# State space stage of a two-layer trunk: the response matrices' loads move from GpSimd's queue into SyncE's, between weights and output matrices

## The chip, the core and the metric

The kernel runs on one core of a Trainium2 chip. Its engines are TensorE (PE; its weight loads are PEld), VectorE (DVE), ScalarE (ACT), GpSimd (POOL) and SyncE (SP), which here only issues transfers. Transfers run on 16 DMA engines. SP issues into a hardware queue (q1 in the profile), POOL into a software queue (q0). The metric is the device time of one execution in microseconds (us), the median over several; less is better.

## The reference

Two layers over 256 positions of width 2048, each of them `x += mixer(norm(x))`, `x += attention_to_memory(norm(x))`, `x += mlp(norm(x))`, and a last norm. The mixer of layer 0 is a gated MLP, that of layer 1 the state space layer that the change is in:

```
u = (h @ w_in).reshape(bsz, seq, 128, 16)        # 128 groups of 16 channels
bu = einsum('gpc,bsgc->sbgp', b_bar, u)          # 64 complex states a group
states[s] = lam_bar * states[s - 1] + bu[s]      # associative scan over the positions
y = einsum('gcp,sbgp->bsgc', cmat, states).real + d_skip * u
y = gelu(y.reshape(bsz, seq, 2048))
val, gate = split(y @ w_out + b_out, 2)
x = x + val * sigmoid(gate)
```

Everything is float32, `w_in` is 2048 x 2048, `w_out` 2048 x 4096.

## The kernel before, in words

**Weights.** Every large matmul streams its weights in chunks of 512 KB (`wload`, line 127, issued by SP into `wraw`, four buffers). ScalarE casts a chunk to `whi` (line 103), VectorE subtracts to get the remainder `wlo` (line 104), and PE multiplies both (`gemm_tok`, line 159). A load waits until VectorE has split the chunk four back, so SP spends most of its time waiting for buffers. Eight chunks make one piece of 512 columns. The state space stage has 32 chunks of `b_w_in` (numbers 0 to 31, four pieces n = 0 to 3) and 64 of `b_w_out` (32 to 95).

**The scan in matrices.** The positions are cut into blocks of 8 (`T`). Inside a block the output is a product with a response matrix (names `Kd` in HBM, `dq` on chip); what crosses a block goes through states: `pq` (from `Pd`) makes a block's contribution to the state, `carry` runs the recurrence over the blocks, and `qq` (output matrices, from `Qd`) makes outputs from states. All three sorts are worked out by VectorE and PE beside layer 0's MLP and stored in HBM. For each column piece n there are four tiles of each: `pq` and `qq` 512 KB, one transfer each; `dq` 320 KB in four transfers of 32, 64, 96 and 128 KB, as the matrix is zero in steps and its zeros are set once (line 1279). The four dq tiles (`resp`) have one buffer each, so dq of piece n waits until PE has read dq of piece n - 1.

**Order.** `self.at(k, f)` has f issued k chunks after the place where it stands; `self.tick` runs after each chunk. `follow(n)` plans for piece n, whose chunks are just through: `inputs` (transposes, copies to `us`, line 1324), `own` (matmuls with pq, line 1337), `states`, `carry`, `outputs(n, 0)` after 14 chunks and `outputs(n, 1)` after 16, each of them 16 blocks' matmuls with dq (line 1384, 32 matmuls) and then with qq (line 1392, 64 matmuls); for pieces 2 and 3 a chunk or so earlier or later. PE takes this work between the chunks of later pieces.

**Queues.** `load` in `s5` issues on POOL, or with `stream` on SP, behind the last weight load that was issued so far (`issue_after(self.fed)`, line 1272). Before, pq and dq go on POOL (line 1274) and qq on SP; dq of piece 0 is asked for at the start of the stage, while layer 0's MLP still runs, that of later pieces 7 or 8 and 9 or 10 chunks behind their piece.

Of the kernel before, what the change touches and what calls it, by code (L numbers as in the profile page):

```python
# [16 lines left out]
P = 128  # L17
# [21 lines left out]
class Trunk:  # L39
# [1219 lines left out]
    def s5(self, x, cur, nxt):  # L1259
# [3 lines left out]
        with tc.tile_pool(name="s5", bufs=2, reuse_waits="tile") as sp:  # L1263
# [5 lines left out]
            def load(src, out, stream=False):  # L1269
                if stream:  # L1270
                    with tc.issue_after(self.fed):
                        nc.sync.dma_start(out=out, in_=src)
                else:
                    nc.gpsimd.dma_start(out=out, in_=src)
# [6 lines left out]
            def fetch(nm, n, i, stream=False):  # L1281


                if nm == "pq":
                    t = sp.tile([P, 2, 4, P], F32, name=nm, bufs=4)
                    load(self.Pd[4 * n + i], t, stream)
                elif nm == "qq":
                    t = sp.tile([P, 2, 4 * P], F32, name=nm, bufs=4)
                    load(self.Qd[4 * n + i].rearrange("l p r n -> (l p) r n"), t, stream)
                else:  # L1290
                    t, kd = resp[i], self.Kd[4 * n + i]
                    for h in range(4):
                        load(bass.AP(tensor=kd.tensor, offset=kd.offset + 6 * P,
                                     ap=[[P, 2], [(2 * T - 1) * P, 16], [1, 2 * (h + 1) * P]]),
                             t[32 * h:32 * h + 32, 2 * (3 - h) * P:])
                ahead[nm, n, i] = t

            def chunks(n, acc):
# [17 lines left out]
            def inputs(n):  # L1316
                u = st[n].pop()
                us = sp.tile([P, 8, 4, NC], F32, name="us")
                st[n] += [us]
                for h in range(2):  # L1320
                    pt = self.ps([P, 4, P])
                    for l in range(4):
                        nc.tensor.transpose(pt[:, l, :], u[:, 4 * h + l].rearrange("p j c -> p (j c)"), self.ident)
                    nc.scalar.copy(out=us[:, 4 * h:4 * h + 4].rearrange("p l t c -> p l (t c)"), in_=pt)

            def own(n):

                us, = st[n]
                z = sp.tile([P, 4, 2, 2, 64], F32, name="z", bufs=1)
                st[n] += [z]  # L1330
                for h in range(2):
                    pz = self.ps([P, 2, 2, 2, 64])
                    for i in range(2):
                        pq = ahead.pop(("pq", n, 2 * h + i))
                        for l in range(2):
                            for t in range(4):
                                nc.tensor.matmul(pz[32 * t:32 * t + 32, i, l].rearrange("p r s -> p (r s)"),
                                                 us[:, 4 * h + 2 * i + l, t, :], pq[:, l, t, :],
                                                 start=(i + l == 0), stop=True, skip_group_check=True)
                    for i in range(2):  # L1340
                        nc.scalar.copy(out=z[:, 2 * h + i], in_=pz[:, i].rearrange("p l r s -> p r l s"))

            def states(n):

                z = st[n].pop()
                vv = sp.tile([P, 2, NC, NQ // 2], F32, name="vv")
                st[n] += [vv]
                nc.vector.memset(vv[:, :, 0, :], 0.0)
                for h in range(2):
                    pt = self.ps([P, 2, 2, 4, NC])  # L1350
                    for i in range(2):
                        for r in range(2):
                            nc.tensor.transpose(pt[:, i, r].rearrange("p t c -> p (t c)"),
                                                z[:, 2 * h + i, r].rearrange("p l s -> p (l s)"), self.ident)
                    for i in range(2):
                        vo = vv[:, :, 1:, :].rearrange("p r c (t l) -> p l r t c", t=4)[:, 2 * h + i]
                        nc.scalar.copy(out=vo, in_=pt[:, i, :, :, 0:NC - 1])

            def carry(n, c, k, by=1):

                vv = st[n][1]
                cs = slice(16 * n, 16 * n + 16)
                p = by // 2
                m1, m2 = (sp.tile([P, 2, 15, 16], F32, name=f"m{i}", bufs=1)[:, :, :k, :] for i in (1, 2))
                at = lambda c, r: vv[:, r, c:c + 2 * by * (k - 1) + 1:2 * by, :]
                t1 = self.TC1[:, p, cs].unsqueeze(1).unsqueeze(1).broadcast_to([P, 2, k, 16])
                t2 = self.TC2[:, p, :, cs].unsqueeze(2).broadcast_to([P, 2, k, 16])
                new = at(c, slice(None))
                nc.vector.tensor_tensor(out=m1, in0=t1, in1=at(c - by, slice(None)), op=ALU.mult)
                nc.vector.tensor_tensor(out=m2, in0=t2, in1=at(c - by, slice(None, None, -1)), op=ALU.mult)  # L1370
                nc.vector.tensor_tensor(out=new, in0=new, in1=m1, op=ALU.add)
                nc.vector.tensor_tensor(out=new, in0=new, in1=m2, op=ALU.add)

            def outputs(n, half):
                us, vv = st[n][:2]
                if half == 0:
                    st[n] += [[self.ps([P, 4, P]) for _ in range(2)]]
                py = st[n][2]
                pair = (2 * half, 2 * half + 1)
                for i in pair:  # L1380
                    dq = ahead.pop(("dq", n, i)).rearrange("p (j t l c) -> p l t j c", j=T, l=2, t=4)
                    for l in range(2):
                        for t in range(4):
                            nc.tensor.matmul(py[l][32 * t:32 * t + 32, i, :], us[:, 2 * i + l, t, :], dq[:, l, t],
                                             start=(i == 0), stop=False, skip_group_check=True)
                for i in pair:
                    qv = ahead.pop(("qq", n, i)).rearrange("p r (j t c) -> p r t j c", t=4, c=16)
                    for r in range(2):
                        for l in range(2):
                            s = slice(64 * l, 64 * l + 64)  # L1390
                            for t in range(4):
                                nc.tensor.matmul(py[l][32 * t:32 * t + 32, i, :], vv[s, r, :, 4 * t + i],
                                                 qv[s, r, t], start=False, stop=(r == 1), skip_group_check=True)
# [18 lines left out]
            def follow(n):  # L1412

                late = n == NCH - 1
                self.at(5 + late, lambda: own(n))
                for i in range(4):
                    if n + 1 < NCH:
                        self.at(5, lambda i=i: fetch("pq", n + 1, i))
                    if n:
                        self.at(7 + late + i // 2 * 2, lambda i=i: fetch("dq", n, i))  # L1420
                        self.at(10 + late + i // 2 * 2, lambda i=i: fetch("qq", n, i, True))
                self.at(4 + late, lambda: inputs(n))
                self.at(6 + late, lambda: states(n))
                self.at(7 + late, lambda: [carry(n, 2, 15), carry(n, 4, 7, 2)])
                self.at(8 + late, lambda: [carry(n, c, 1, 4) for c in (8, 12, 16)])
                self.at(9 + late, lambda: [carry(n, c, 1, 4) for c in (20, 24, 28)])
                self.at(10 + late, lambda: [carry(n, 6, 7, 2), carry(n, 3, 15)])
                gap = n == NCH - 2
                self.at(14 + 1.5 * gap, lambda: outputs(n, 0))
                self.at(16 + gap, lambda: outputs(n, 1))  # L1430
                self.at(16 + gap, lambda: activated(n))
                self.at(17 + gap if n >= NCH - 2 else 19, lambda: features(n))

            for i in range(4):
                fetch("pq", 0, i)
            for i in range(4):
                fetch("dq", 0, i)
                self.at(2 * i + 2, lambda i=i: fetch("qq", 0, i, True))
            for n in range(NCH):
                acc = self.gemm_tok(hT, a["b_w_in"], n)  # L1440
                if n == 0:
                    st["rstd"] = cur.rstd()
                chunks(n, acc)
                follow(n)
# [224 lines left out]
```

## Time and profile before

| what | value |
|---|---|
| median of 3 runs | 2770.2 us (2769.85 to 2771.99) |
| profiled execution | 2772.35 us |
| its span | 2770.2 us |
| granted TensorE clock | 0.999 |
| TensorE busy | 2748.3 us, 99% |
| VectorE, ScalarE, GpSimd busy | 2066.9, 1426.7, 184.9 us |
| DMA | 593.75 MB, mean 214 GB/s |
| state space stage: chunk 0 to 46 | about 1385 to 1548 us |

The span is the time from the first to the last instruction of the profiled execution; times in the rows are from its start. "PE ps L1384 <- DMA dq<-Kd" reads: PE, in the instruction of line 1384 that writes `ps`, waited for the transfer of `Kd` to `dq`. In a row of the timeline stand start, length, engine, line, operation, output and inputs, shapes, how many, and in brackets the idle time before it with what ended it. In a row of the transfers stand their number, the size of one and the median time from issue to landing; "SPq" and "POOLq" say on which queue.

### The profile page before, as it was taken

The page shows a single profiled execution, that of the slowest core. Times are in us where ns is not written, and L with a number is a line of the kernel's source. Part 1 is how long each engine was busy: PE and PEld are TensorE (multiplying, and loading weights), DVE is VectorE, ACT ScalarE, POOL GpSimd, SP SyncE. Part 2 cuts the span into 40 slices and gives each one's busy share as a digit, 9 for nine tenths or more (in the row PEclk, how much of TensorE's full clock was granted, in tenths as well). Part 3 has the DMA queues.
Part 4 walks back from the last instruction along what each step waited for, and adds up shares of the span by engine and source line. Part 5 has one row for each costly group of instructions (what it writes and reads, how often), then busy time and mean ns, then how long its engine had stood idle before and what let it go on. Part 6 is the DMA issues. An engine that isn't in the chain of part 4 may idle for free. (4 is left out here: it accounts for less than half of the span.)

```text
span 2770.2 us, 39500 instructions
## 1 busy us (share of the span) xinstructions
PE 2748.3 (99%) x14966; PEld 2325.4 (84%) x14966; DVE 2066.9 (75%) x2835; ACT 1426.7 (51%) x1822; POOL 184.9 (7%) x331
## 2 busy tenths in 40 slices
PE   9999999999999999999999999999999999999998
PEld 7888888888888888888888788888888888888887
DVE  6865757878888878787577657568767978879685
ACT  5545545655544434444566445446555655546454
POOL 0100000001011111111203100000000000000000
PEclk9999999999999999999999999999999999999999
DMA  8766566457688887886879766564556557575565
GB/s 293 231 199 214 189 193 217 152 160 238 211 281 259 262 258 257 265 259 219 235 239 284 207 203 206 188 213 156 181 165 231 180 171 241 158 246 166 176 212 160
DMA packets 194175, 593.75 MB, mean 214 GB/s; under 512 B 44096, under 2 KB 45168, under 8 KB 193472
## 3 DMA queue, kind: packets, MB, share of 16 engines
q1 hardware_dynamic: 153456, 537.46, 61.1%
q0 software_dynamic: 40000, 52.71, 6.6%
q8 instruction: 117, 1.92, 0.3%
q10 hardware_dynamic: 528, 1.06, 0.1%
q14 instruction: 74, 0.61, 0.1%
HBM read 567.51 MB, written 23.46 MB: 213 GB/s over the span
## 5 line engine op out<-in xcount | busy, mean ns | idle before, releaser
L104 DVE TENSOR_TENSOR wlo<-wraw,whi 128x1024 fp32r<-128x1024 f32 (+1 forms) x857 | 1041.0, 1220 | 434.8 <-ACT whi L103 429.0
L103 ACT CAST whi<-wraw 128x1024 fp32r<-128x1024 f32 (+1 forms) x857 | 899.4, 1051 | 800.2 <-PE acc L910 172.1
L174 PE MATMUL acc<-act,whi 128*128 128x512 f32 x3072 | 740.9, 391 | 0.6 <-DVE act L246 0.6
L174 PEld LDWEIGHTS acc<-act,whi 128*128 128x128 f32 x3072 | 563.1, 188 | 110.6 <-issue 1.4
L179 PEld LDWEIGHTS acc<-act,wlo 128*128 128x128 f32 x3072 | 395.0, 191 | 17.4 <-DVE wlo L104 1.8
L179 PE MATMUL acc<-act,wlo 128*128 128x256 f32 x3072 | 403.3, 283 | 1.3 <-DVE wlo L104 1.0
L159 PE MATMUL acc<-whi,act 128*128 128x512 f32 x1472 | 370.4, 393 | 5.6 <-ACT whi L103 5.5
L159 PEld LDWEIGHTS acc<-whi,act 128*128 128x128 f32 x1472 | 275.2, 189 | 63.6 <-ACT whi L103 6.3
L810 PE MATMUL acc<-whi,act 128*128 128x512 f32 x824 | 222.7, 392 | 0.0
L910 PE MATMUL acc<-whi,hl 128*128 128x512 f32 x544 | 212.7, 391 | 0.0
L909 PE MATMUL acc<-whi,hh 128*128 128x512 f32 x544 | 212.6, 391 | 0.0
L159 PE MATMUL acc<-wlo,act 128*128 128x512 f32 x736 | 197.9, 391 | 0.0
L810 PEld LDWEIGHTS acc<-whi,act 128*128 128x128 f32 x824 | 152.9, 188 | 35.9 <-ACT ends L846 2.2
L159 PEld LDWEIGHTS acc<-wlo,act 128*128 128x128 f32 x736 | 138.6, 188 | 28.9
L912 PE MATMUL acc<-wlo,hh 128*128 128x512 f32 x544 | 145.8, 389 | 0.0
L810 PE MATMUL acc<-wlo,act 128*128 128x512 f32 x412 | 127.2, 391 | 0.2
L190 ACT COPY r<-acc 128x512 f32<-128x512 f32 x64 | 37.6, 587 | 161.9 <-PE acc L174 161.9
L910 PEld LDWEIGHTS acc<-whi,hl 128*128 128x128 f32 x544 | 102.1, 188 | 22.2 <-issue 1.0
L810 PE MATMUL acc<-whi,hh 128*128 128x512 f32 x308 | 120.5, 391 | 0.0
L909 PEld LDWEIGHTS acc<-whi,hh 128*128 128x128 f32 x544 | 102.1, 188 | 21.4 <-issue 0.2
L912 PEld LDWEIGHTS acc<-wlo,hh 128*128 128x128 f32 x544 | 102.0, 188 | 21.4 <-issue 0.2
L810 PE MATMUL acc<-whi,hl 128*128 128x512 f32 x308 | 119.9, 389 | 0.0
(387 smaller groups left out, 2951.3 us busy)
## 6 DMA issues: line engine op xcount, KB each, us to landing
wraw<-in_f_w_up SPq DMA_DIRECT2D x256, 512.0 KB, 4.5
wraw<-in_f_w_down SPq DMA_DIRECT2D x200, 512.0 KB, 5.6
wraw<-in_x_w_q SPq DMA_DIRECT2D x64, 512.0 KB, 3.7
wraw<-in_x_w_k SPq DMA_DIRECT2D x64, 512.0 KB, 4.5
wraw<-in_b_w_out SPq DMA_DIRECT2D x64, 512.0 KB, 4.5
wraw<-in_a_w_in SPq DMA_DIRECT2D x63, 512.0 KB, 4.7
wraw<-in_x_w_o SPq DMA_DIRECT2D x48, 512.0 KB, 4.3
wraw<-in_x_w_v SPq DMA_DIRECT2D x40, 512.0 KB, 3.9
```

The lines of the kernel that those rows point to most:

```text
L103: self.nc.scalar.copy(out=hi, in_=src)
L104: return self.nc.vector.tensor_tensor(out=lo, in0=src, in1=hi.bitcast(F32), op=ALU.subtract).ins
L159: nc.tensor.matmul(out[t], a[:, kt, sl], b[:, kk, :], start=st and a is ah, stop=en)
L174: nc.tensor.matmul(acc[:, f, :], hi[:, kk, sl], both[:, kt].rearrange("p a s -> p (a s)"), start=first and kk == 0, stop=last and kk == FK ...
L179: nc.tensor.matmul(acc[:, f, 0:S], lo[:, kk, sl], ah[:, kt, :], start=False, stop=last and kk == FK - 1, skip_group_check=True)
L190: nc.scalar.copy(out=dst, in_=acc[:, :, S:])
L810: mm = lambda s, m, e: nc.tensor.matmul(out, s, m, start=key not in begun, stop=e, skip_group_check=True)
L909: nc.tensor.matmul(acc[:, t, :], ah, hi[:, kk, :], start=kt == 0, stop=False)
L910: nc.tensor.matmul(acc[:, t, :], al, hi[:, kk, :], start=False, stop=False)
L912: nc.tensor.matmul(acc[:, t, :], hid[kt // 4][0][:, kt % 4, sl], lo[:, kk, :], start=False, stop=kt == KT - 1)
```

## The change

The transfers of dq go through `load` with `stream`, so on SP. For pieces 1 to 3 they are asked for 12 and 14 chunks behind the piece, with qq one chunk behind each pair. For piece 0 the four dq tiles are asked for at chunks 6, 8, 14 and 16 and the four qq tiles at 9, 11, 17 and 19.

```diff
@@ fetch
                 else:
                     t, kd = resp[i], self.Kd[4 * n + i]
                     for h in range(4):
-                        load(bass.AP(tensor=kd.tensor, offset=kd.offset + 6 * P,
+                        load(stream=stream, src=bass.AP(tensor=kd.tensor, offset=kd.offset + 6 * P,
                                      ap=[[P, 2], [(2 * T - 1) * P, 16], [1, 2 * (h + 1) * P]]),
-                             t[32 * h:32 * h + 32, 2 * (3 - h) * P:])
+                             out=t[32 * h:32 * h + 32, 2 * (3 - h) * P:])
@@ follow
-                    if n:
-                        self.at(7 + late + i // 2 * 2, lambda i=i: fetch("dq", n, i))
-                        self.at(10 + late + i // 2 * 2, lambda i=i: fetch("qq", n, i, True))
+                for k, nm in enumerate(("dq", "qq")) if n else ():
+                    for i in range(4):
+                        self.at(12 + i // 2 * 2 + k, lambda nm=nm, i=i: fetch(nm, n, i, True))
@@ s5, ahead of the pieces
-            for i in range(4):
-                fetch("dq", 0, i)
-                self.at(2 * i + 2, lambda i=i: fetch("qq", 0, i, True))
+            for k, nm in enumerate(("dq", "qq")):
+                for i in range(4):
+                    self.at((6, 8, 14, 16)[i] + 3 * k, lambda nm=nm, i=i: fetch(nm, 0, i, True))
```

What it moves on SP's queue for piece 0, behind the first six weight chunks of `b_w_in` (each row a transfer, "x6" six alike, the tile's number behind its name, out and in, and the output's shape in float32 elements):

```order
 L127 DMA wraw<-in_b_w_in 128x1024 x6
+L1272 DMA dq_12413<-Kd_5680 32x1x256
+L1272 DMA dq_12413<-Kd_5680 32x1x512
+L1272 DMA dq_12413<-Kd_5680 32x1x768
+L1272 DMA dq_12413<-Kd_5680 32x1x1024
+L127 DMA wraw<-in_b_w_in 128x1024 x2
+L1272 DMA dq_12414<-Kd_5681 32x1x256
+L1272 DMA dq_12414<-Kd_5681 32x1x512
+L1272 DMA dq_12414<-Kd_5681 32x1x768
+L1272 DMA dq_12414<-Kd_5681 32x1x1024
+L127 DMA wraw<-in_b_w_in 128x1024
 L1272 DMA qq<-Qd_5664 128x1024
```

The first two dq tiles now stand between weight chunks 5 and 8, and the first output matrix behind chunk 8 instead of chunk 5.

On the same queue for piece 2, at the start of `b_w_out`:

```order
-L127 DMA wraw<-in_b_w_in 128x1024 x2
-L127 DMA wraw<-in_b_w_out 128x1024 x5
+L127 DMA wraw<-in_b_w_in 128x1024
+L127 DMA wraw<-in_b_w_out 128x1024 x4
+L1272 DMA dq_12413<-Kd_5688 32x1x256
+L1272 DMA dq_12413<-Kd_5688 32x1x512
+L1272 DMA dq_12413<-Kd_5688 32x1x768
+L1272 DMA dq_12413<-Kd_5688 32x1x1024
+L1272 DMA dq_12414<-Kd_5689 32x1x256
+L1272 DMA dq_12414<-Kd_5689 32x1x512
+L1272 DMA dq_12414<-Kd_5689 32x1x768
+L1272 DMA dq_12414<-Kd_5689 32x1x1024
```

Eight dq transfers now stand ahead of chunk 36 (the fifth of `b_w_out`), and eight more ahead of chunk 38; the same holds for chunks 28 and 30 with piece 1, while for piece 3 all sixteen, with two qq among them, stand ahead of chunk 46.

ScalarE's order changes in two places; the first is in piece 2, where a cast of a weight chunk (line 103) stood ahead of the copies to us:

```order
 L103 CAST act<-ps 128x4x4x32 x2
-L103 CAST whi<-wraw 128x1024
 L1324 COPY us<-ps 128x512 x2
 L103 CAST whi<-wraw 128x1024
 L1341 COPY z<-ps 128x256 x4
-L103 CAST whi<-wraw 128x1024
+L103 CAST whi<-wraw 128x1024 x2
 L1357 COPY vv<-ps 128x2x4x31 x4
```

The copies to us stand one cast earlier now; in piece 3 they do too. PE's and VectorE's instructions keep their order, and POOL's queue loses the 64 transfers of dq.

## Prediction, on record before the changed kernel ran

> **What bounds the kernel now.** I read the page first, then what TensorE (PE) waits for in the state space stage, then the timeline at its one long wait, and last the transfers.
>
> ```profile
> span 2770.2 us, 39500 instructions
> PE 2748.3 (99%) x14966; PEld 2325.4 (84%) x14966; DVE 2066.9 (75%) x2835; ACT 1426.7 (51%) x1822; POOL 184.9 (7%) x331
> q1 hardware_dynamic: 153456, 537.46, 61.1%
> q0 software_dynamic: 40000, 52.71, 6.6%
> ```
>
> PE is the bound: 21.9 us of the span are without a matmul. The profiled execution took 2772.35 us, 2.15 around its span and 2.15 above the median of 2770.2; I work out a difference against it and add that to the median. A difference under 0.2% (5.5 us) can't be told from none. Over the whole span the hardware queue moved 537.46 MB on 61.1% of 16 engines: 537.46 / (0.611 x 16 x 2770.2 us) = 19.8 GB/s for an engine while it is busy.
>
> The change touches 1386 to 1560 us. All that PE waits for from 1380 to 1640 (us in total, times, longest):
>
> ```profile
> PE ps L1384 <- DMA dq<-Kd: 2.5, 2, 1.9
> PE ps L1337 <- ACT us L1324: 1.7, 2, 0.9
> PE ps L1323 <- ACT u L1312: 0.4, 1, 0.4
> ```
>
> So at most 4.6 us of waiting can go. The first row is one place, the second half of the last column piece's outputs:
>
> ```profile
> 1546.06 1.08 PE L1384 MATMUL ps<-dq,us 128*32 128x128 f32 x32
> 1547.07 1.21 PE L1392 MATMUL ps<-qq,vv 64*32 64x128 f32 x64
> 1548.22 2.11 PE L159 MATMUL ps<-whi,act 128*128 128x512 f32 x8
> 1550.16 1.07 PE L159 MATMUL ps<-wlo,act 128*128 128x512 f32 x4
> 1551.07 1.98 PE L159 MATMUL ps<-whi,act 128*128 128x512 f32 x8
> 1552.88 1.07 PE L159 MATMUL ps<-wlo,act 128*128 128x512 f32 x4
> 1554.56 0.65 PE L1384 MATMUL ps<-dq,us 128*32 128x128 f32 x16 [0.61 <-DMA dq<-Kd]
> 1557.06 0.80 PE L1384 MATMUL ps<-dq,us 128*32 128x128 f32 x16 [1.85 <-DMA dq<-Kd]
> 1557.79 1.96 PE L1392 MATMUL ps<-qq,vv 64*32 64x128 f32 x64
> 1559.68 2.63 PE L159 MATMUL acc<-whi,act 128*128 128x512 f32 x8
> 1562.15 1.07 PE L159 MATMUL acc<-wlo,act 128*128 128x512 f32 x4
> 1563.06 1.04 PE L1407 MATMUL ps<-ident,y 128*128 128x128 f32 x8
> ```
>
> From 1552.88 to 1563.06 are 10.18 us. The undisturbed half before needs 1548.22 - 1546.06 = 2.16 for its outputs, a chunk's whi and wlo matmuls 1551.07 - 1548.22 = 2.85, and the opening wlo group about 0.99 of that: 6.00 in all. The wait costs 4.18: 2.46 of standing and 1.7 of slower matmuls behind it (the same 64 qq matmuls 1.96 against 1.21). The clock shows it:
>
> ```profile
> core 0: us, PE busy (x) PEld busy (x) DVE busy (x) ACT busy (x) POOL busy (x), PEclk, DMA share, GB/s
> 1515.00:1546.00 31.00, 30.38 (x368) 24.70 (x368) 23.03 (x51) 14.53 (x23) 9.98 (x17) 1.00 0.95 249
> 1546.00:1563.00 17.00, 14.54 (x229) 11.27 (x229) 3.68 (x3) 4.89 (x6) 0.00 (x0) 0.90 0.64 193
> ```
>
> **The change, part by part.** *Moved bytes.* A dq tile is four transfers of 32, 64, 96 and 128 KB: 320 KB, sixteen tiles, 64 transfers, 5120 KB. They leave POOL's queue and stand in SyncE's (SP's) between weights.
>
> ```profile
> Qd<-room POOLq DMA_DIRECT2D x32, 256.0 KB, 12.0
> Pd<-room POOLq DMA_DIRECT2D x32, 256.0 KB, 6.2
> pq<-Pd POOLq DMA_DIRECT2D x16, 512.0 KB, 7.8
> dq<-Kd POOLq DMA_DIRECT2D x16, 32.0 KB, 13.0
> q0 software_dynamic: 1208, 0.64, 15.4%
> ```
>
> The last column is the time to landing. Qd and Pd are written from the same queue in the same size; Qd's pattern has 2 as its slowest dimension, Pd's 128, and Qd takes twice as long. The source pattern of dq begins with a dimension of 2 too (`[P, 2]`), and its 32 KB land later than pq's 512. The last row is from 1537 to 1557 us, where dq alone is on POOL's queue: 0.64 MB busy 15.4% of 16 engines, 2.5 engines. I read that as two engines to a transfer, while a weight chunk of 512 KB uses all sixteen, 32 KB on each.
>
> On POOL, transfers of this kind go beside the weights. On SP they go ahead of weights in the same order, and a weight chunk has landed only when its share on the two engines has. What transfers with a small slowest dimension do to weights on SP can be seen at lb (slowest dimension 8), whose loads stand between the weights of layer 0's MLP and not of layer 1's; the first row is from 1000 to 1290 us, the second from 2200 to 2480:
>
> ```profile
> wraw<-in_f_w_up SPq DMA_DIRECT2D x64, 512.0 KB, 6.4
> wraw<-in_f_w_up SPq DMA_DIRECT2D x61, 512.0 KB, 3.8
> ```
>
> That is 2.6 us later, where 32 KB take 1.65 at 19.8 GB/s: what an lb of 256 KB on eight engines, 32 KB on each, would add if its engines' weights stood behind it. Which engines a piece takes on SP no row of before shows; I take the same two each time, and leave the other case to the rivals. The Trainium skill ("DMA: Bandwidth & Descriptors", "Why a DMA increments its semaphore by 16 and not by 1") states this rule: a copy runs on the largest number up to 16 that divides the slowest dimensions of both sides, on a hardware queue always the lowest-numbered engines, on GpSimd's a turning choice. By it the two engines here are fixed and the time is the sum below; the traces so far show the number of engines, not which.
>
> *The sum for the two engines.* From the first dq (behind the sixth weight of b_w_in, issued at about 1386.7) to the load of chunk 46, the last behind the dq's, each of the two moves, in KB: dq 5120 / 2 = 2560; 41 weights x 32 = 1312; 14 qq x 32 = 448; 12 pq x 32 = 384. Together 4704 KB, 4.82 MB. PE wants chunk 46 at 1548.22, its cast and landing 1.1 earlier.
>
> ```profile
> 1386.68 1.29 SPq L1272 DMA_DIRECT2D qq<-Qd  x3
> 1497.62 0.33 SPq L127 DMA_DIRECT2D wraw<-in_b_w_out  x1
> 1503.76 23.54 SPq L127 DMA_DIRECT2D wraw<-in_b_w_out  x8
> GB/s 348 348 338 402 397 437 368 398 328 358 246 259 258 200 219 229 214 219 224 291 318 286 279 293 254 301 259 234 226 221 197 195 189 195 314 293 273 263 377 407
> ```
>
> There are 1547.1 - 1386.7 = 160.4 us for it. At 19.8 GB/s the 4.82 MB need 243 us (+83). The last row (1454 to 1487 us) has fast slices of 397 to 437 GB/s, 24.8 to 27.3 an engine: 194 us (+34) and 177 (+16). I take 24.8, because the fourteen other engines mostly stand still while the two work off their backlog. The backlog is not there all the time: between chunk 39's load at 1497.6 and the dq's of the last piece at some 1525 stand only weights, seven of 32 KB, 9 us of work in 25. Up to 16 us of forced rest can be added there; nothing at the lower end, since the backlog from ahead may fill it; I take 9, about half.
>
> *Clock.* Each long wait is followed by slower matmuls, 1.7 us above. I expect about five places where PE stops (chunks 16, 30, 36, 38 and 46, each right behind dq's): +8, from +3 for fewer.
>
> *What goes.* The wait for dq, -4.2: dq(3) is now asked for at the twelfth chunk and lands ahead of the weight behind it, for which PE waits anyway. The two waits for us, 0.9 each, -1.8: ScalarE copies us a cast earlier for the last two pieces, and does so with weights late too.
>
> *Issue.* SP has 64 more transfers to issue; a transfer of lb's kind takes 0.63 us there, 40 us in all:
>
> ```profile
> L1168 SPq DMA_DIRECT2D lb<-in_b_pc x32: 615/627/741, 718.2 to 1240.9; - x32
> SPq L127 <- DVE wlo L104: 285.4, 110, 8.9
> POOL dq L1274 <- DMA dq<-Kd: 41.6, 21, 4.8
> POOL dq L1274 <- PE ps L1384: 9.4, 4, 6.4
> ```
>
> SP stands 285.4 of the 350 us from 1500 to 1850 waiting for a free weight buffer, so 40 cost nothing there; if that cover goes, up to 5 us for one set of 8 transfers. POOL loses 64 issues and 41.6 us of waits; nothing but dq and two biases waits for it. Behind the eight dq's in a row on SP stand weights and qq; a full queue of 8 in flight (what POOL's row above shows) stops the weight's issue until the first has landed. That is part of the backlog, not added. The later qq (ticks 13 and 15) has room as long as its neighbours do, and the outputs that want it come behind a weight that is later: nothing added. A dq also waits until PE has read the tile's last content, on SP now with the weights behind it; on POOL that was 6.4 us at the longest, and dq is asked for four to five chunks later (over 11 us): nothing. The first piece's dq no longer load beside the MLP's last weights, where PE did not wait for DMA: nothing.
>
> Sum: +34 + 9 + 8 - 4.2 - 1.8 = +45, 2815 us (2817 for the profiled execution). Ends: +16 + 0 + 3 - 6 = +13 (2783), and +83 + 16 + 8 - 6 = +101 (2871).
>
> **The rivals.**
>
> *The pieces spread on SP, and the waits go.* If successive pieces fall on different engines, they share the 16 with the weights as now, only asked for earlier. For it: on POOL the last set, 1.31 MB from its first issue at 1525.05 to the end of PE's wait at 1557.06, came at 41 GB/s, two engines' worth, beside weights that stayed in time. Then all three waits go: -4.18 - 1.8 = -6.0, 2764.2. It decides if a weight lands within the 11.4 us (4 buffers x 2.85) that its load is ahead.
>
> ```profile
> 1525.05 4.70 POOL L1274 DMA_DIRECT2D dq<-Kd  x8 [6.41 <-PE ps L1384]
> 1545.10 0.59 POOL L1274 DMA_DIRECT2D dq<-Kd  x1 [2.22 <-DMA dq<-Kd]
> ```
>
> *Only the dq wait goes, or it is hidden.* The queue's change moves the wait by what issuing takes, and new small waits eat the us part: between -4.2 and +1, 2766 to 2771. The Trainium skill (the same page, "Issuing engines are not separate DMA queues") says that another issuing engine saves only its time to issue, since all end on the same 16 engines; that is this case. Against it: the shared order above.
>
> *Only the limit of 8 in flight delays the weights.* Eight pieces in a row are 640 KB; at 41 GB/s 16 us, against a lead of 11.4: up to 4.6 late, at each of the six groups of the last three sets, +28 at most, halved since qq and weights between them shorten the lead only in part: +14 - 6 = +8, 2778. It decides if a group lands later than 11.4 us.
>
> **How the numbers follow.** The two engines with the order of the weights: 0.74, 2815, own range 2783 to 2871 with 0.62 of the whole in it. Limit of 8 alone: 0.11, 2778 (2773 to 2787). Only the dq wait or nothing: 0.09. All waits gone: 0.06. For 8 in 10 the range reaches down into the third rival, and to half of what lies above 2871: 2775 to 2878. Faster by over 0.2% (below 2764.7) 0.06; within 0.2% (to 2775.7) 0.10; slower 0.84.
>
> **What the changed profile would show.** Right: ScalarE's casts of in_b_w_in and in_b_w_out waiting many us for their transfer, PE waiting for whi or wlo at line 159 behind chunks 16, 30, 36, 38 and 46, a granted clock under 1 there, a low DMA share in those stops, no wait at line 1384, weights landing in over 10 us between 1400 and 1600. Forecast wrong: weights landing in under 8 us there (the pieces spread; 2764), or stops of a few us at SP waiting for dq with a high DMA share (limit of 8). If the stops are there but half as long, the engine's rate was mis-sized; if a stop comes beside line 1384 or 1392, dq or qq themselves are too late.

## The result, and the profile after

The changed kernel takes 2842.1 us (median of 5, 2841.2 to 2843.8) against 2769.9 on the same chip: ratio 1.0262, interval 1.0247 to 1.0277, some 72 us slower. The forecast was 2815 (2775 to 2878). The profiled execution took 2842.09 us with a span of 2840.0. One of the four executions of the run with eight engines below was slow (4969.8 us at a granted clock of 0.745) and is left out there; every other time here is of fast executions.

The page of the changed kernel, busy times and DMA queues:

```profile
span 2840.0 us, 39517 instructions
PE 2762.4 (97%) x14966; PEld 2334.4 (82%) x14966; DVE 2067.2 (73%) x2835; ACT 1426.3 (50%) x1822; POOL 146.9 (5%) x267
PEclk9999999999999999999998799999999999999999
q1 hardware_dynamic: 155632, 542.71, 60.3%
q0 software_dynamic: 29760, 47.41, 5.6%
```

The same number of matmuls now counts 14.1 us more of busy time: PE ran part of them with a lower clock (0.987 in the mean, 0.999 before). The 5.2 MB of dq have gone from q0 to q1. What PE waits for in the stage, 1380 to 1720 us (us in total, times, longest):

```profile
PE ps L159 <- ACT whi L103: 15.1, 1, 15.1
PE ps L1337 <- ACT us L1324: 14.4, 3, 12.5
PE ps L1353 <- ACT z L1341: 12.8, 1, 12.8
PE acc L159 <- ACT whi L103: 7.3, 3, 2.9
PE ps L1323 <- ACT u L1312: 4.5, 3, 2.7
PE acc L159 <- ACT u L1312: 4.2, 1, 4.2
PE ps L1392 <- issue: 1.6, 1, 1.6
```

59.9 us in all, 4.6 before. With the 14.1 of slower matmuls, 55.3 + 14.1 = 69.4 of the 69.8 us by which the span grew. All rows but one name ScalarE, and no row names a transfer; dq at line 1384 is gone. ScalarE's own waits show what it stood for, and its timeline at the stop of 12.8 us shows how that reaches PE:

```profile
ACT whi L103 <- DMA wraw<-in_b_w_in: 53.2, 11, 19.9
ACT whi L103 <- DMA wraw<-in_b_w_out: 50.9, 8, 24.1
...
1519.49 1.04 ACT L103 CAST whi<-wraw 128x1024 fp32r<-128x1024 f32 x1 [19.86 <-DMA wraw<-in_b_w_in]
1520.45 1.19 ACT L1341 COPY z<-ps 128x256 f32<-128x256 f32 x4
```

The cast of chunk 30 waited 19.86 us for its weights, and the copy to z, ready long before, stood behind it on ScalarE. PE needed z first and so is booked as waiting for z. All three long stops are of this kind or the plain one: behind the loads of chunk 30 (12.8 us), 38 (12.5, at us) and 46 (15.1, at whi).

The transfers from 1590 to 1618 us, ahead of the last stop and in it, in 40 slices of 0.7 us (DMA: busy tenths of 16 engines):

```profile
DMA  2992111111111211111178999999999999996111
GB/s 75 382 293 75 60 53 56 47 53 53 47 59 47 72 48 50 53 48 54 50 205 269 275 272 304 298 331 272 278 281 246 260 272 281 234 257 164 59 53 53
```

For twelve us one to two tenths of the engines are busy and move some 53 GB/s: two engines at 26.5. SP has at this time only transfers of the last piece in flight, dq and what is left of two qq between them, up to eight together:

```profile
1588.75 12.23 SPq L1272 DMA_DIRECT2D dq<-Kd  x8
1601.08 2.32 SPq L127 DMA_DIRECT2D wraw<-in_b_w_out  x1
```

Were they on different engines, more than two would be busy. The weights of chunk 46 are issued at 1601.08, behind them, the cast can start at 1618.48, and PE's stop of 15.1 us ends at 1619.58:

```profile
1618.48 1.04 ACT L103 CAST whi<-wraw 128x1024 fp32r<-128x1024 f32 x1 [24.14 <-DMA wraw<-in_b_w_out]
1619.58 3.78 PE L159 MATMUL ps<-whi,act 128*128 128x512 f32 x8 [15.11 <-ACT whi L103]
```

The trace also keeps when the parts of a transfer report that they have landed. On SP's queue a weight chunk leaves sixteen such events; a dq transfer leaves three, one between 1 and 2 us after its issue and two later. That reads as one for each engine, and an early one for the engines without a part. (In the runs below, dq transfers with a slowest dimension of 8 leave nine, with 16 or 32 sixteen.) The events around chunk 46:

| transfer | parts landed, us |
|---|---|
| last dq but one ahead of chunk 46 (96 KB) | 1613.21, 1613.87 |
| last dq ahead of it (128 KB) | 1616.78, 1617.13 |
| chunk 46, fourteen parts | 1606.50 to 1607.47 |
| chunk 46, last two parts | 1617.96, 1618.38 |

Its last two parts land behind the dq's, 10.9 us after the fourteenth. At chunk 30 the fourteen had landed by 1504.08 and the two by 1519.42, at chunk 38 by 1556.82 and 1568.20. In the kernel before, the last part of a weight chunk issued from 1386 to 1560 us comes at most 2.0 us behind the fourteenth.

By the Trainium skill ("DMA: Bandwidth & Descriptors", "Why a DMA increments its semaphore by 16 and not by 1") the engines of such a transfer are two and, on a hardware queue, the same ones each time; the two busy engines with up to eight transfers in flight agree, and so do the two late parts of each chunk.

### The profile page after: what moved, and what is told of

Same layout as the page of the kernel before. It is cut to its first block, busy times and chain, and to the rows that moved or that the text cites. A ratio compares the mean times of both kernels' runs of the same rounds, so it can differ in the third digit from the quotient of the medians.

```text
span 2840.0 us, 39517 instructions
## 1 busy us (share of the span) xinstructions
PE 2762.4 (97%) x14966; PEld 2334.4 (82%) x14966; DVE 2067.2 (73%) x2835; ACT 1426.3 (50%) x1822; POOL 146.9 (5%) x267
## 4 chain that ended last, share of the span: by engine, by line
PE 81%; DMA 6%; DVE 2%; ACT 1%; issue 0%; SPq 0%; DVEq 0%; ACTq 0%
PE acc L174 24%; PE acc L810 22%; PE acc L179 13%; PE acc L159 5%; PE acc L910 4%; PE acc L912 4%; PE acc L909 4%; DMA wraw<-in_b_w_in 2%; DMA wraw<-in_b_w_out 2%; PE ps L532 1%; PE ps L644 1%; DVE wlo L104 1%; PE ps L159 1%; DMA qq<-Qd 0%; DMA dq<-Kd 0%; PE ps L236 0%
## 5 line engine op out<-in xcount | busy, mean ns | idle before, releaser
L159 PE MATMUL acc<-whi,act 128*128 128x512 f32 x1472 | 378.2, 400 | 17.2 <-ACT whi L103 13.0
L159 PEld LDWEIGHTS acc<-whi,act 128*128 128x128 f32 x1472 | 279.9, 192 | 77.7 <-ACT whi L103 14.4
L810 PE MATMUL acc<-whi,act 128*128 128x512 f32 x824 | 222.5, 392 | 0.0
```

Of the source, the lines that this page charges most:

```text
L159: nc.tensor.matmul(out[t], a[:, kt, sl], b[:, kk, :], start=st and a is ah, stop=en)
L810: mm = lambda s, m, e: nc.tensor.matmul(out, s, m, start=key not in begun, stop=e, skip_group_check=True)
```

## The experiments

The theory: on SP each dq transfer takes the same two engines, because its slowest dimension is 2, and stands there ahead of the weights' share. Rival 1: SP's limit of eight transfers in flight holds the weights back, by the number of transfers. Rival 2: the later places of dq and qq in the order cost the time. All comparisons are with the kernel before on the same chip.

**The order alone.** dq stays on POOL's queue, everything else as changed, but for ScalarE's order, which is that of the kernel before.

```diff
-                        load(stream=stream, src=bass.AP(...
+                        load(src=bass.AP(...
```

> Changed kernel's places in the order (dq 12 and 14 chunks behind a piece, qq at 13 and 15, piece 0 at 6 to 19), but dq stays on POOL's queue. Theory (two engines): POOL's queue is not the weights', so no stop; as before within some us, 2764 to 2778, with waits for dq at line 1384 if any. Rival 1 (limit of 8 on SP): also as before, 2764 to 2778. Rival 2 (the order): 2835 to 2845.

2769.6 us, ratio 0.9995 (0.9986 to 1.0004): no difference. Rival 2 is out; the places cost nothing, and gain nothing either. (The changed order on ScalarE costs nothing either: the run on plain rows and the one with the doubled store on SP have it, and are without the 72 us.)

**Sixteen engines by twice the transfers.**

```diff
-                        load(stream=stream, src=bass.AP(... ap=[[P, 2], [(2 * T - 1) * P, 16], [1, 2 * (h + 1) * P]]),
-                             out=t[32 * h:32 * h + 32, ...])
+                        for l in range(2):
+                            load(stream=stream, src=bass.AP(... ap=[[(2 * T - 1) * P, 16], [1, 2 * (h + 1) * P]]),
+                                 out=t[32 * h + 16 * l:32 * h + 16 * l + 16, ...])
```

> Changed kernel, each dq transfer cut in two of 16 partitions, whose slowest dimension is 16 on both sides: 128 transfers on SP's queue, same bytes, same places. Theory (each dq transfer of the changed kernel runs on the same two engines, in order ahead of the weights there): now every engine carries 320 + 1312 + 448 + 384 = 2464 KB, 2.52 MB, up to chunk 46, where the two had 4.82 MB; at the 20.6 GB/s that the changed kernel's stage gave (4.82 MB in 234 us) 122 us of 160, so no stop: 2763 to 2771 us. Rival 1 (SP's limit of 8 transfers in flight holds the weights back, by number): twice the transfers, so at least as slow as the changed kernel, 2840 or more. Rival 2 (the later places of dq and qq in the order, whatever carries them): 2835 to 2845 as the changed kernel.

2803.0 us, ratio 1.0113 (1.0098 to 1.0128): between both. More than half of the loss is gone though the number of transfers doubled, against rival 1, but 33 us remain, against the theory's 2763 to 2771. The build had made another order of VectorE's, ScalarE's and PE's work for this kernel, and its timeline shows that order at work. ScalarE at the first stop, with the helper's line numbers one higher:

```profile
1397.80 1.05 ACT L103 CAST whi<-wraw 128x1024 fp32r<-128x1024 f32 x1 [1.67 <-PE acc L159]
1407.80 1.22 ACT L1313 ACTIVATE u<-acc,rstd 32x128 f32<-32x128 f32 x4 [8.95 <-DVE u L1310]
1409.05 1.04 ACT L103 CAST whi<-wraw 128x1024 fp32r<-128x1024 f32 x1
```

The cast at 1409.05 waits for no transfer; it stands behind activations for u that wait 8.95 us for VectorE, three casts earlier in the order than in the changed kernel. No late engines are left: a weight chunk's last part lands at most 2.0 us behind the fourteenth. That the order costs the 33 us is the likely reading, but no run shows it; this one does not separate order and number.

**Eight engines, a quarter of the transfers.** Each dq tile in one transfer, zeros with it.

```diff
-                    for h in range(4):
-                        load(stream=stream, src=bass.AP(... offset=kd.offset + 6 * P, ap=[[P, 2], ...
+                    load(stream=stream, src=bass.AP(tensor=kd.tensor, offset=kd.offset,
+                                 ap=[[P, 8], [(2 * T - 1) * P, 16], [1, T * P]]), out=t)
```

> Changed kernel, each dq tile as one transfer of 512 KB, zeros included (slowest dimension 8): 16 transfers on SP, 8192 KB instead of 5120. Theory (number of engines from the slowest dimension, always the same ones): eight engines carry 8192/8 + 1312 + 448 + 384 = 3168 KB, 3.24 MB, at 20.6 GB/s 157 us of 160: on the edge, no long stop, 2764 to 2785. Rival 1 (limit of 8, by number): a quarter of the transfers, little or no stop, 2764 to 2790. Rival 2 (order): 2835 to 2845. If one engine or two carried it all: over 2900.

2803.0 us, ratio 1.0108 (1.0089 to 1.0127): 18 us over the theory's upper end, 13 over rival 1's. PE's and VectorE's order is that of the changed kernel and ScalarE's that of the kernel before, so this remainder is no matter of order. It comes the way the theory says, on eight engines: a dq transfer leaves one landing event and eight later, and of chunk 46 eight parts land by 1556.60, the other eight from 1570.46 to 1572.02. Then the cast starts:

```profile
1572.12 1.04 ACT L103 CAST whi<-wraw 128x1024 fp32r<-128x1024 f32 x1 [16.71 <-DMA wraw<-in_b_w_out]
```

From the first dq at 1383.68 the 3.24 MB on each of the eight took 188 us, 17.2 GB/s: the path was as the theory had it, and the rate of 20.6 was too high here. One stretch of low rate is where dq of the second piece loads; the columns are us, busy time of PE, PEld, DVE, ACT and POOL, clock, DMA share and GB/s:

```profile
1462.00:1471.00 9.00, 9.00 (x124) 7.39 (x115) 8.45 (x36) 5.85 (x12) 0.00 (x0) 1.00 1.02 183
```

All sixteen engines are busy, yet 183 GB/s are moved, 11.4 an engine. Why they are slower there (the eight engines read overlapping parts of one tile's store) was not tested.

**The same number, wider.** The pattern with 2 ahead, each transfer as wide as the tile.

```diff
-  offset=kd.offset + 6 * P, ap=[[P, 2], [(2 * T - 1) * P, 16], [1, 2 * (h + 1) * P]]), out=t[32 * h:32 * h + 32, 2 * (3 - h) * P:])
+  offset=kd.offset + 2 * h * P, ap=[[P, 2], [(2 * T - 1) * P, 16], [1, T * P]]), out=t[32 * h:32 * h + 32, :])
```

> Changed kernel with its 64 transfers and patterns of slowest dimension 2, each as wide as the whole tile (128 KB, zeros included): 8192 KB instead of 5120, same number, same places. Theory (two engines): these carry 8192/2 + 1312 + 448 + 384 = 6240 KB, 6.39 MB, at 20.6 GB/s 310 us of 160: +150, less where the rest of the queue fills rests, 2890 to 2930. Rival 1 (limit of 8, by number): as the changed kernel, 2835 to 2855. Rival 2 (order): 2835 to 2845.

2897.2 us, ratio 1.0456 (1.0438 to 1.0473): +127, inside the theory's range; by number it should have stayed at 2835 to 2855. The build changed the order here too, which in the run with 128 transfers went along with 33 us, less than the 55 between this run and the changed kernel. And PE now waits for dq itself too (line 1384, here 1383), from 1380 to 1720 us:

```profile
PE acc L159 <- ACT whi L103: 53.1, 6, 19.9
PE ps L1383 <- DMA dq<-Kd: 38.7, 4, 12.5
```

The next four keep PE's and VectorE's order; ScalarE's is the changed kernel's in the first two and that of the kernel before in the last two, which differ in two places. So no other order of work stands between them and the kernels before and after.

**The same number, size and place, plain rows.**

```diff
-                    t, kd = resp[i], self.Kd[4 * n + i]
+                    t, kd = resp[i], self.Qd[4 * n + i]
...
-                                     ap=[[P, 2], [(2 * T - 1) * P, 16], [1, 2 * (h + 1) * P]]),
+                                     ap=[[T * P, 32], [1, 2 * (h + 1) * P]]),
```

> Changed kernel, order of all engines' work kept; the 64 dq transfers keep number, size and place, but read 32 plain rows of the output matrices' store instead of the response matrices (slowest dimension 32 on both sides), so the response matrices are left out. Theory (two engines carry all dq): every engine carries 320 + 2144 = 2464 KB, 2.52 MB, 122 us of 160 at 20.6 GB/s: no stop behind dq, 2763 to 2772. Rival 1 (SP's limit of 8 in flight, by number; the run with 128 transfers was 33 us over before): 2800 to 2845. Rival 3 (in that run it was the other order of ScalarE's and VectorE's work, which the build made of 128 transfers): 2763 to 2775 here.

2766.2 us, ratio 0.9987 (0.9979 to 0.9996). Only the pattern's slowest dimension (32 in place of 2) and the bytes' place in HBM differ from the changed kernel, and all 72 us are gone; a weight chunk's last part lands at most 2.5 us behind the fourteenth. Rival 1, the limit by number alone, is out. It also shows that sixteen engines to a transfer do not by themselves cost the rest of the run with 128 transfers.

**A valid kernel of this kind.** The response matrices are stored twice, the second copy shifted by a block, so that 32 rows have one stride.

```diff
-                nc.gpsimd.dma_start(out=self.Kd[m][:, :, t], in_=kds[m % 2][32 * t:32 * t + 16])
+                for c in range(2): nc.gpsimd.dma_start(out=self.Kd[m][16 * c:16 * c + 16, 0:NL - c, t],
+                                                       in_=kds[m % 2][32 * t:32 * t + 16, c:])
...
-                                     ap=[[P, 2], [(2 * T - 1) * P, 16], [1, 2 * (h + 1) * P]]),
+                                     ap=[[(2 * T - 1) * P, 32], [1, 2 * (h + 1) * P]]),
```

> Changed kernel with the response matrices stored twice in HBM, the second copy shifted by one block, so that each of the 64 transfers reads 32 rows of one stride (slowest dimension 32); 64 more writes of 28 KB on POOL's queue beside layer 0's MLP. Theory: as the run that reads plain rows, and the waits of before for dq and us gone, 2763 to 2772. Rival 1: 2800 to 2845.

2765.5 us, ratio 0.9982 (0.9973 to 0.9991): faster than the kernel before by about 4 us. Of PE's waits one row is left from 1380 to 1720 us, and dq lands in 3 to 7 us:

```profile
span 2763.9 us, 39649 instructions
PE ps L1323 <- ACT u L1312: 0.2, 1, 0.2
dq<-Kd SPq DMA_DIRECT2D x16, 128.0 KB, 4.0
dq<-Kd SPq DMA_DIRECT2D x16, 32.0 KB, 6.7
```

Its span is 6.3 us shorter than before, in the profiled executions; the rival "all waits go" had said 6.0. The medians differ by 4.4.

**The same store, on POOL.** The kernel before, its order and queues, with the doubled store.

> Kernel before (dq on POOL's queue, its order) with the doubled store and transfers of slowest dimension 32. Theory (two engines to a transfer is why a dq lands in 13 us): landing falls to under 10 us, the wait of 2.5 us at line 1384 and its slow clock go, 2765 to 2769. Rival (dq waits for its tile or for POOL's order): no change, 2769 to 2771.

2766.5 us, ratio 0.9987 (0.9978 to 0.9996), as fast as the last one. On POOL too the number of engines sets the landing of dq: 7.3 us for 32 KB and 6.9 for 128 from 1380 to 1560, where both took 13.8 in the kernel before. The first two rows are of this run, the last two of the kernel before:

```profile
dq<-Kd POOLq DMA_DIRECT2D x12, 128.0 KB, 6.9
dq<-Kd POOLq DMA_DIRECT2D x12, 32.0 KB, 7.3
dq<-Kd POOLq DMA_DIRECT2D x12, 128.0 KB, 13.8
dq<-Kd POOLq DMA_DIRECT2D x12, 32.0 KB, 13.8
```

So the queue did not matter once the pattern spreads.

**Half the bytes on the two engines.**

```diff
-  ap=[[P, 2], [(2 * T - 1) * P, 16], [1, 2 * (h + 1) * P]]), out=t[32 * h:32 * h + 32, 2 * (3 - h) * P:])
+  ap=[[P, 2], [(2 * T - 1) * P, 16], [1, (h + 1) * P]]), out=t[32 * h:32 * h + 32, 2 * (3 - h) * P:(7 - h) * P])
```

> Changed kernel with its pattern of slowest dimension 2 and its 64 transfers, each of half the width: 2560 KB instead of 5120; half of every response matrix is left out. Theory: the two engines carry 1280 + 2144 = 3424 KB, 3.5 MB, 170 us of 160 at 20.6 GB/s: +10 and the clock, 2770 to 2792. Rival 1 (by number): 2835 to 2845.

2782.1 us, ratio 1.0043 (1.0030 to 1.0055): +12, as the theory had it, at an unchanged number of transfers. (Half of each response matrix is left out.) The last part of a weight chunk lands up to 5.1 us behind the fourteenth here, in the changed kernel up to 15.3. The three doses in MB on each of the two engines and their cost: 3.5 for +12, 4.82 for +72, 6.39 for +127. From the first to the second that is 60 us for 1.31 MB, 21.9 GB/s an engine. From the second to the third it is 55 for 1.57, 28.5, more than the 26.5 that the two moved alone; with another order and waits for dq itself that step gives no rate.

## Why the prediction was right or wrong

**The mechanism was right.** The row of Qd against Pd (12.0 and 6.2 us for the same size) and the 2.5 engines of POOL's queue were read as two engines to a transfer; the run on plain rows and the one with the doubled store show that this pattern, on this queue, costs the time. That the same two are taken on SP was a choice then; the slices at 53 GB/s and the two late parts of each chunk, in order behind the dq's, show it.

**The queue's time was too small.** The prediction took 24.8 GB/s an engine, "because the fourteen other engines mostly stand still", and 9 us of rest. From the first dq on SP to the cast of chunk 46 the 4.82 MB took 1618.48 - 1384.16 = 234 us, 20.6 GB/s, rests included. The first dq went out 2.5 us earlier than the 1386.7 of the prediction, so 162.9 us were there for it.

```profile
1384.16 2.60 SPq L1272 DMA_DIRECT2D dq<-Kd  x4
```

The reason was half right: alone the two run at 26.5 each. But when SP can issue again, the weights and qq held back start on all sixteen, and the row of slices above then has 234 to 331 GB/s, 15 to 21 an engine. The value that was left at the upper end, 19.8, the mean over the whole span, was the better one: measured, the term is 1618.48 - 1547.1 = +71, not +43. That is the step that was mis-sized.

**The clock was too small, and not a term by itself.** +8 were forecast, 14.1 measured. The columns below are as above:

```profile
1385.00:1482.00 97.00, 85.20 (x651) 68.13 (x650) 56.79 (x117) 46.68 (x87) 4.21 (x8) 0.95 0.68 212
1482.00:1580.00 98.00, 64.93 (x559) 52.01 (x557) 45.93 (x107) 38.74 (x76) 2.08 (x4) 0.81 0.58 172
1580.00:1640.00 60.00, 44.89 (x538) 36.02 (x537) 26.22 (x55) 16.36 (x20) 0.00 (x0) 0.86 0.51 159
```

Up to chunk 46 the two engines set the end, and a slower matmul there only shortens the next stop: queue and clock should not have been added in full. What adds is the clock behind the last stop. PE starts chunk 46 at 1619.58 instead of 1548.22, 71.4 us later; from there to line 1407 it needs 1632.83 - 1619.58 = 13.25 us, against 1563.06 - 1548.22 = 14.84 before, of which 4.18 were the cost of the wait for dq: 2.6 more.

```profile
1632.83 1.04 PE L1407 MATMUL ps<-ident,y 128*128 128x128 f32 x8
```

71.4 + 2.6 - 4.2 = 69.8, the span's growth.

**The stops.** Long ones came at 30, 38 and 46 as said; at 16 and 36 they were short (2.9 and 4.2 us), and one at chunk 8 (2.5) was not foreseen. PE's rows name whi at 46, 16, 17 and 8, but u at 36, z at 30 and us at 38. The weights landed late, as said (22 us after their issue at chunk 30, 18 and 17 at 38 and 46), but the sign "a low DMA share in those stops" failed. The three long stops:

```profile
1508.30:1521.14 12.84, 0.00 (x1) 0.00 (x1) 0.57 (x1) 1.65 (x4) 0.00 (x0) 0.53 0.76 242
1557.41:1569.88 12.47, 0.00 (x1) 0.00 (x1) 0.51 (x1) 1.58 (x3) 0.00 (x0) 0.61 0.69 190
1604.47:1619.58 15.11, 0.00 (x1) 0.01 (x1) 0.02 (x1) 1.04 (x1) 0.00 (x0) 0.62 0.79 217
```

The share is 0.69 to 0.79: first all sixteen work on what was held back (at chunk 30 on pq from POOL's queue too), and only the last few us show two engines alone. The low share (0.14 from 1592.2 to 1604) comes ahead of the stop.

**What goes.** The dq wait went (-4.2), as said. The wait for us (-1.8) did not: "and does so with weights late too" was wrong, since the copies stand behind a cast that waits for its weights, and PE now waits 14.4 us for us. In the repaired kernel, where weights are in time, both waits went.

**The rivals.** That only the dq wait goes (0.09) is out by the measured time. That the limit of eight alone delays the weights (0.11) had slow pieces in it too, so the run on plain rows, whose pieces are fast, does not decide it; its price, +8 and at most +28, was too low, and the landings speak against it: a late issue delays all sixteen parts, but the fourteen had landed before PE stopped at chunks 30 and 38 (1508.30 and 1557.41) and 3.0 us behind the start of the stop at 46. What the limit adds by letting the weights it holds back run beside the two engines' last pieces was not separated. That all waits go (0.06) is what happens when the pattern spreads, though not in the way that rival had it, by pieces on different engines.

## What to carry to other kernels

Before a transfer is moved into the queue that feeds the bound engine, look at the slowest dimension of its pattern: with a small one, few engines carry it, and everything behind it in that queue waits for these engines. Reckon the bytes on the busiest engine up to a due time, not the mean, and with the rate under load. A layout in HBM that gives the load one stride of many rows was worth more than the choice of queue: with it both queues were 3 to 4 us faster than before.

## What the runs showed that was not expected

Sixteen busy engines moved only 183 GB/s while a tile's overlapping rows were read by eight of them (the run with eight engines), where the kernel before moves 280 and 298 at the same share:

```profile
1453.00:1482.00 29.00, 28.13 (x350) 22.94 (x352) 23.85 (x58) 18.12 (x34) 9.75 (x17) 1.00 1.01 280
1482.00:1515.00 33.00, 32.81 (x352) 26.54 (x341) 25.02 (x59) 19.39 (x38) 10.80 (x19) 1.00 1.01 298
```

And splitting the transfers, 128 in place of 64, made the build put the casts of weights behind other work, which came along with a loss of 33 us; making them wider at the same number changed the order too. A change of the transfers alone can change the order on engines that have no part in it.
